# Four token-major projections in 512-column chunks, with their weights in a pool opened behind the ssd mixer

## The chip, the core and the metric

The kernel runs on one core of one Trainium2 chip. The metric is the device time of one launch in microseconds (us). The kernel before takes 2990.47 us, the median of three runs (2987.92 to 2991.99).

On a core, PE multiplies matrices, DVE does element-wise vector work, ACT does functions and copies, POOL does small odd jobs, and SP, ACT and POOL put DMAs into queues. Each engine works through its own list in order. A list may stop at a semaphore until another engine or a DMA has finished.

## The reference, cut to what matters

The reference is two transformer blocks in sequence over 1024 tokens of width 1024. The first has an RWKV-7 branch, a differential attention branch and a mixture of experts. The second, which the change touches, is this:

```python
h = rms_norm_2(x, pre_norm_w[l])
proj = h @ w_in[l]
z, xbc, dt_raw, q, f_raw, i_in, g, u, s5_gate = jnp.split(proj, splits, axis=-1)
y_ssd = ssd_mixer(z, xbc, dt_raw, ...)
y_hgrn = hgrn2_mixer(q, f_raw, i_in, g, ...)
y_s5 = s5_mixer(u, s5_gate, ...)
mix = jnp.concatenate([y_ssd, y_hgrn, y_s5], axis=-1)
x = x + rms_norm_2(mix @ w_out[l], post_norm_w[l])
```

The columns `i_in`, `g`, `u` and `s5_gate` are 512 wide each. Their products with `h` are the four products I0, G0, U0 and SG0 of the title; `g` and `s5_gate` pass through a SiLU.

## The kernel before, in words

All products keep float32 accuracy by splitting each operand into a high part (fp32r, made by a copy on ACT) and a low part (the difference, made on DVE). `mm3` then issues three matmuls for each block of 128 input rows: lines 262, 263 and 264. A product over 1024 input rows has 8 such blocks, so it takes 24 matmuls for each output tile.

`load_w` (line 208) brings weights in. For each part of `part` blocks it loads a raw tile by SP (`wr`, line 220, tag `wraw`), copies the high part on ACT (`wh`, line 181) and subtracts on DVE (`wl`, line 182). Each tag has a number of buffers; a new tile takes the buffer of an old one once all readers of that one are done.

The second block's input `h` lies transposed in SBUF as `hU` (high and low). There are two kinds of product with it:

- Feature-major (`proj_fm`, and the conv products of `ssd`): the output has features on partitions, and a matmul streams 512 tokens of `hU` past 128 columns of weights. The trace writes it `mm<-hU,wh`.
- Token-major (`proj_tm`, and the Z products of `ssd`): the output has 128 tokens on partitions, and a matmul streams CW columns of weights past 128 tokens of `hU`. The trace writes it `mm<-wh,hU`. With CW = 256, a product 512 wide is two chunks of 8 token tiles of 24 matmuls.

A chunk's weights are two parts of four blocks (128x1024 each), in a pool `wq` that all products of this stage share: two raw buffers and two each of `wl` and `wh`, which is one chunk.

`mixers` writes the second block in this order: `ssd` (conv products, Z products, and then a scan over eight chunks of 128 tokens, which is called chunk 0 to 7 below), then F0 and Q0 (feature-major), I0 and G0 (token-major), then the first three of four `hgrn` heads with U0 behind the first and SG0 behind the second, then the s5 mixer with the last head and the output projection.

That is the order of the program's text. The order on each engine is made when the program is built: a scheduler simulates the program and lets each engine take, of the instructions that are ready in its simulation, the one that the text has first. So instructions of the scan stand between those of F0, Q0, I0 and G0. Once built, the order on an engine is fixed, whatever the real times are.

One scan chunk is mostly DVE work. In turn: `y` from line 1408, then for each of two groups of eight heads the decay matrix `dec` (eight instructions of line 1418 on a loaded tile, exp on ACT at line 1419, a product with the scores from PE, line 1421, at line 1423), eight small matmuls with it (line 1426), a product with the state (line 1430), which DVE scales into `yo` (line 1432) and adds (lines 1433, 1434), an update of the state (matmul of line 1437, DVE lines 1439 and 1440), a gate (1443) with a sum of squares on ACT (1444). At the end of the chunk come a power on POOL (line 177), the scaling of `y` (line 1450), eight transposes on PE (line 1453), copies on ACT (line 1456) and a store. Lines 1406 and 1407 prepare the next chunk's `xdt` and `xw`.

Tiles live in pools that are opened and closed like a stack. The scan's pools (`sd_one` with its constants and the tokens `x_tm`, and `sd_wk`) are opened above `wq` and closed at the end of `ssd`.

Of the kernel before, what the change touches and what calls it, by code (L numbers as in the profile page):

```python
# [1458 lines left out]


LEVELS = (64, 32, 16, 8, 4, 2, 1)
CW = 256


def proj_tm(K, hT, wp, pool, c0, n, dst, silu=False):

    nc = K.nc
    for c in range(n // CW):
        w = K.load_w(wp, K.ap["w_in_2"][0], [(c0 + c * CW, CW)], raw_bufs=2)
        for j in range(8):  # L1470
            p = K.gemm_tm(w, hT, j, CW)
            z = pool.tile([128, CW], F32, name=K.name("pz"), tag="stage", bufs=3)
            evac(K, z, p[:, :CW], silu)
            nc.sync.dma_start(dst[j * 128:(j + 1) * 128, c * CW:(c + 1) * CW], z)


def proj_fm(K, hT, wp, pool, c0, n, dst, silu=False):

    nc = K.nc
    for f in range(n // 128):  # L1480
        w = K.load_w(wp, K.ap["w_in_2"][0], [(c0 + f * 128, 128)], part=KT, raw_bufs=2)
        for hf in range(2):
            p = K.gemm_fm(w, 0, 128, hT, hf * 512)
            z = pool.tile([128, 512], F32, name=K.name("pz"), tag="stage", bufs=3)
            evac(K, z, p, silu)
            nc.sync.dma_start(dst[f * 128:(f + 1) * 128, hf * 512:(hf + 1) * 512], z)


def evac(K, z, p, silu):
    if silu:  # L1490
        K.nc.scalar.activation(z, p, AF.Tanh, scale=0.5)
        K.nc.vector.scalar_tensor_tensor(z, z, 1.0, p, op0=OP.add, op1=OP.mult)
    else:
        K.nc.scalar.activation(z, p, AF.Copy)
# [540 lines left out]
def final_first(K, es, mixT_d, part_d):  # L2035


    nc = K.nc
    KF = 8
    fp = es.enter_context(K.pool(name="f1", bufs=1))  # L2040
    mv = mixT_d.rearrange("(k p) t -> p k t", p=128)
    for c in range(2):
        cs = slice(c * 512, (c + 1) * 512)
        w = K.resident(fp, K.ap["w_out_2"][0], 0, KF, cs, "f1w", raw_bufs=2)
        for j in range(8):
            rows = slice(j * 128, (j + 1) * 128)
            raw = fp.tile([128, KF, 128], F32, name=K.name("fr"), tag="fr", bufs=2)
            m = [fp.tile([128, KF, 128], F32R, name=K.name(f"fm{i}"), tag=f"fm{i}", bufs=2) for i in range(2)]
            nc.sync.dma_start(raw, mv[:, :, rows])
            K.split(m[0], m[1], raw)  # L2050
            p = K.gemm_tm(w, m, 0, 512, kt=KF)
            y = fp.tile([128, 512], F32, name=K.name("fy"), tag="fy", bufs=1)
            nc.scalar.activation(y, p, AF.Copy)
            nc.scalar.dma_start(part_d[rows, cs], y)
            yield
# [105 lines left out]
def mixers(K, es, hT, d5, mixT_d, part_d, x3_d, out):  # L2161

    tc = K.tc
    with K.pool(name="md", bufs=1, space=DRAM) as dd:
        wp, pool = [es.enter_context(K.pool(name=n, bufs=1)) for n in ("wq", "wqs")]
        dt = lambda n, *s: dd.tile(list(s), F32, name=f"d_{n}")
        zs_d, f_d, q_d, v_d = dt("zs", T, 1024), dt("f", 512, T), dt("q", 512, T), dt("v", T, 512)
        gh_d, u_d, g5_d = dt("gh", T, 512), dt("u", T, 512), dt("g5", T, 512)  # L2170
        ssd(K, hT, wp, pool, zs_d, mixT_d[0:1024, :], s5_tables(K, d5))
        a = (K, hT, wp, pool)
        proj_fm(*a, F0, 512, f_d)
        proj_fm(*a, Q0, 512, q_d, silu=True)
        proj_tm(*a, I0, 512, v_d)
        proj_tm(*a, G0, 512, gh_d, silu=True)
        heads = hgrn(K, f_d, q_d, v_d, gh_d, mixT_d[1024:1536, :])
        for h in range(3):
            next(heads)
            if h == 0:  # L2180
                proj_tm(*a, U0, 512, u_d)
            if h == 1:
                proj_tm(*a, SG0, 512, g5_d, silu=True)
        es.close()
        fs = ExitStack()
        last = Final(K, fs)
        first = final_first(K, fs, mixT_d[0:1024, :], part_d)

        def go(n, behind):
            with tc.issue_after(behind.ins):  # L2190
                for _ in range(n):
                    next(first)

        for _ in range(3):
            next(first)
        states = s5(K, d5, u_d, g5_d, last.open)
        next(states)
        next(heads)
        next(heads, None)
        for n in (2, 2, 2, 4):  # L2200
            next(states)
            go(n, K.last)
        for _ in states:
            mm = K.last
        end = last.run(mixT_d[1024:1536, :], part_d, x3_d, out)
        next(end)
        go(3, mm)
        next(end, None)
        fs.close()


def program(tc, nc, cst, out, **ap):
# [32 lines left out]
    pps.close()  # L2245
    rings.close()
    mixers(K, es, hT, d5, mixT_d, part_d, x3_d, out)
    K.close()

# [13 lines left out]
```

## Time and profile before

| | |
|---|---|
| time, median of three | 2990.47 us (2987.92 to 2991.99) |
| profiled execution | 2983.03 us |
| its span in the trace | 2981.3 us |
| PE busy | 2806.6 us, 94% |
| DVE busy | 1965.1 us, 66% |
| ACT busy | 1315.6 us, 44% |
| mean granted PE clock | 0.967 of full |

Matmuls are pipelined: each is longer than the distance to the next, so the busy time of PE is not its rate. The distance from start to start is. Times are read from the span's start. The second block begins near 2000 us, F0 runs from about 2265 us, Q0 ends at 2370.65 us, I0 and G0 follow until about 2497.5 us, U0 and SG0 until about 2641 us, and s5 and the output projection take the rest.

### The profile page before, as it was taken

What the parts mean: (1) busy time and instruction counts of PE and PEld (TensorE: products, weight loads), DVE (VectorE), ACT (ScalarE), POOL (GpSimd) and SP (SyncE); (2) the same over time, 40 slices, a digit from 0 to 9 for tenths busy, and PEclk for the clock granted to TensorE, in tenths of its full rate; (3) what the DMA queues carried; (4) which work ended last, traced back from release to release, by engine and by line L of the source; (5) the groups of instructions that cost most, each with busy time, mean ns of one, the idle gap of its engine ahead of it and who ended that gap; (6) DMA issues with size and microseconds to landing.
All of it is one profiled execution on the core that took longest, in us unless ns stands there. A gap on an engine that the chain in (4) does not pass through costs nothing. (4 is left out here: it accounts for less than half of the span.)

```text
span 2981.3 us, 47275 instructions
## 1 busy us (share of the span) xinstructions
PE 2806.6 (94%) x18410; PEld 2303.9 (77%) x18410; DVE 1965.1 (66%) x3826; ACT 1315.6 (44%) x2167; POOL 237.0 (8%) x193
## 2 busy tenths in 40 slices
PE   5999999998999989879999999899999999999998
PEld 4878888775777768668877777678888899987776
DVE  4436678744454655669989888469844676768653
ACT  3222223223454321568877878334432335543441
POOL 0000111100000000101222120000000000000000
PEclk9999999997899999889999999999999999999999
DMA  5333334323121655779999998442324444347333
GB/s 162 106 94 96 87 114 126 99 70 119 54 64 54 239 154 182 252 247 380 378 360 334 349 366 288 165 138 82 97 95 143 131 127 144 100 151 234 116 124 131
DMA packets 378146, 503.31 MB, mean 169 GB/s; under 512 B 86039, under 2 KB 234422, under 8 KB 377918
## 3 DMA queue, kind: packets, MB, share of 16 engines
q1 hardware_dynamic: 347742, 458.63, 46.7%
q0 software_dynamic: 11296, 24.57, 2.3%
q10 hardware_dynamic: 18880, 17.05, 1.7%
q8 instruction: 146, 2.39, 0.3%
q14 instruction: 82, 0.67, 0.1%
HBM read 410.26 MB, written 106.68 MB: 173 GB/s over the span
## 5 line engine op out<-in xcount | busy, mean ns | idle before, releaser
L182 DVE TENSOR_TENSOR wh<-we,wh 128x1024 fp32r<-128x1024 f32 x384 | 451.3, 1220 | 61.4 <-ACT wh L181 60.1
L181 ACT ACTIVATE wh<-we 128x1024 fp32r<-128x1024 f32 x384 | 386.1, 1057 | 50.0 <-PE b L264 29.7
L262 PE MATMUL mm<-wh,hU 128*128 128x256 f32 (+1 forms) x768 | 222.9, 292 | 6.8 <-DVE z L1363 4.1
L263 PE MATMUL mm<-wl,hU 128*128 128x256 f32 (+1 forms) x768 | 221.5, 289 | 2.5 <-DVE wl L182 2.5
L264 PE MATMUL mm<-wh,hU 128*128 128x256 f32 (+1 forms) x768 | 219.7, 287 | 0.0
L264 PE MATMUL mm<-wh,hT 128*128 128x256 f32 (+1 forms) x640 | 213.7, 335 | 0.0
L262 PE MATMUL mm<-wh,hT 128*128 128x256 f32 (+1 forms) x640 | 206.0, 338 | 2.7 <-ACT ye L1060 2.3
L262 PE MATMUL mm<-hT,wh 128*128 128x512 f32 x480 | 197.0, 410 | 4.4 <-DVE edge L309 4.2
L181 ACT ACTIVATE wh<-wr 128x1024 fp32r<-128x1024 f32 (+2 forms) x102 | 100.9, 992 | 208.4 <-PE mm L263 156.9
L264 PE MATMUL mm<-hT,wl 128*128 128x512 f32 x480 | 192.5, 401 | 0.0
L263 PE MATMUL mm<-hT,wh 128*128 128x512 f32 x480 | 192.1, 400 | 0.0
L182 DVE TENSOR_TENSOR wl<-wr,wh 128x1024 fp32r<-128x1024 f32 (+2 forms) x102 | 116.0, 1139 | 111.2 <-ACT wh L181 103.9
L262 PEld LDWEIGHTS mm<-wh,hU 128*128 128x128 f32 x768 | 147.2, 193 | 11.0 <-DVE z L1363 5.1
L263 PEld LDWEIGHTS mm<-wl,hU 128*128 128x128 f32 x768 | 148.0, 193 | 5.7 <-DVE wl L182 3.3
L264 PEld LDWEIGHTS mm<-wh,hU 128*128 128x128 f32 x768 | 148.0, 193 | 1.4 <-issue 1.4
L262 PEld LDWEIGHTS mm<-wh,hT 128*128 128x128 f32 x640 | 123.5, 194 | 21.5 <-issue 4.3
L264 PEld LDWEIGHTS mm<-wh,hT 128*128 128x128 f32 x640 | 124.0, 194 | 12.7 <-issue 1.5
L262 PE MATMUL mm<-hU,wh 128*128 128x512 f32 x320 | 128.5, 402 | 4.5 <-ACT wh L181 4.5
L263 PE MATMUL mm<-hU,wh 128*128 128x512 f32 x320 | 127.7, 399 | 0.0
L264 PE MATMUL mm<-hU,wl 128*128 128x512 f32 x320 | 126.9, 397 | 0.0
L262 PEld LDWEIGHTS mm<-hT,wh 128*128 128x128 f32 x480 | 92.5, 193 | 31.7 <-ACT xs L303 4.5
L263 PE MATMUL mm<-wl,hT 128*128 128x256 f32 x384 | 114.0, 297 | 1.3 <-DVE wl L182 1.3
(704 smaller groups left out, 7091.1 us busy)
## 6 DMA issues: line engine op xcount, KB each, us to landing
we<-w_gate SPq DMA_DIRECT2D x64, 1024.0 KB
we<-w_up SPq DMA_DIRECT2D x64, 1024.0 KB
we<-w_down SPq DMA_DIRECT2D x64, 1024.0 KB
wr<-w_in SPq DMA_DIRECT2D x86, 512.0 KB
d_gate<-gz SPq DMA_DIRECT2D x32, 256.0 KB
gt<-d_gate SPq DMA_DIRECT2D x16, 512.0 KB
x<-d_x SPq DMA_DIRECT2D x16, 512.0 KB
dec<-sd_cum SPq DMA_DIRECT2D x16, 512.0 KB
```

What stands on the lines that cost most here:

```text
L181: self.nc.scalar.activation(hi, src, AF.Copy)
L182: self.nc.vector.tensor_sub(lo, src, hi.bitcast(F32))
L262: nc.tensor.matmul(out, a[0], b[0], start=first, stop=False)
L263: nc.tensor.matmul(out, a[0], b[1], start=False, stop=False)
L264: self.last = nc.tensor.matmul(out, a[1], b[0], start=False, stop=last)
```

## The change

CW becomes 512, so that each of the four products is one chunk: 8 token tiles of 24 matmuls of 512 columns. A part is now two blocks of 512 columns (128x1024 again), a chunk has four parts, and `wl` and `wh` get four buffers each; the raw tiles keep two. The pool `wq` is closed behind Q0, and a new pool `wt` is opened for the four products. So that `wq` can be closed on its own, the pool of the output stage tiles (`wqs`) is opened ahead of it.

```diff
-CW = 256
+CW = 512
...
     for c in range(n // CW):
-        w = K.load_w(wp, K.ap["w_in_2"][0], [(c0 + c * CW, CW)], raw_bufs=2)
+        w = K.load_w(wp, K.ap["w_in_2"][0], [(c0 + c * CW, CW)], raw_bufs=2, bufs=4, part=2)
...
-        wp, pool = [es.enter_context(K.pool(name=n, bufs=1)) for n in ("wq", "wqs")]
+        pool = es.enter_context(K.pool(name="wqs", bufs=1))
+        ws = ExitStack()
+        wp = ws.enter_context(K.pool(name="wq", bufs=1))
...
         proj_fm(*a, F0, 512, f_d)
         proj_fm(*a, Q0, 512, q_d, silu=True)
+        ws.close()
+        a = (K, hT, es.enter_context(K.pool(name="wt", bufs=1)), pool)
         proj_tm(*a, I0, 512, v_d)
         proj_tm(*a, G0, 512, gh_d, silu=True)
```

The build of the program places the instructions anew. Four places show it. The number behind a name tells tiles apart; `mm_22470` is the last output tile of Q0, and the lines of the scan are those named above.

On PE before, from within the first tile of I0 (`mm_22511`), right behind Q0: the transposes of chunk 3 stand in the middle of the tile.

```order
L262 MATMUL mm_22511<-wh_22502,hU_17959 128x256
L263 MATMUL mm_22511<-wl_22500,hU_17959 128x256
L264 MATMUL mm_22511<-wh_22502,hU_17960 128x256
L1453 MATMUL t_21554<-c_ident,y_21473 128x128 [waits DVE_49,PE_49]
L1453 MATMUL t_21554<-c_ident,y_21473 128x128 x3
L1453 MATMUL t_21566<-c_ident,y_21473 128x128 [waits DVE_49]
L1453 MATMUL t_21566<-c_ident,y_21473 128x128 x3
L262 MATMUL mm_22511<-wh_22508,hU_17959 128x256 [waits Activation_49]
L263 MATMUL mm_22511<-wl_22506,hU_17959 128x256 [waits DVE_49]
```

On PE now, from the end of Q0 (`mm_22470`): the same transposes, and behind them chunk 4, of which the first ten rows are shown.

```order
L264 MATMUL mm_22470<-hU_17959,wl_22436 128x512
L1453 MATMUL t_21554<-c_ident,y_21473 128x128 [waits DVE_49,PE_49]
L1453 MATMUL t_21554<-c_ident,y_21473 128x128 x3
L1453 MATMUL t_21566<-c_ident,y_21473 128x128 [waits DVE_49]
L1453 MATMUL t_21566<-c_ident,y_21473 128x128 x3
L1421 MATMUL t_21598<-sd_c_fm,sd_b_fm 128x128 [waits Activation_49]
L1437 MATMUL t_21616<-xw_21578,sd_b_tm 128x512 [waits Activation_49]
L1426 MATMUL b_21601<-xdt_21577,dec_21587 128x64 [waits DVE_49]
L1426 MATMUL b_21601<-xdt_21577,dec_21587 128x64 x7
L1430 MATMUL b_21610<-prev_21479,sd_c_fm 128x512
L1421 MATMUL t_21633<-sd_c_fm,sd_b_fm 128x128 [waits PE_49]
L1437 MATMUL t_21651<-xw_21578,sd_b_tm 128x512 [waits DVE_49]
```

It goes on like this through chunks 4, 5, 6 and 7, with no product between. The next piece of PE now is the end of chunk 7 and the first two tiles of I0 (`mm_22527` and `mm_22555`).

```order
L1453 MATMUL t_21969<-c_ident,y_21897 128x128 [waits DVE_49]
L1453 MATMUL t_21969<-c_ident,y_21897 128x128 x3
L1453 MATMUL t_21981<-c_ident,y_21897 128x128 [waits DVE_49]
L1453 MATMUL t_21981<-c_ident,y_21897 128x128 x3
L262 MATMUL mm_22527<-wh_22506,hU_17959 128x512 [waits Activation_49]
L262 MATMUL mm_22555<-wh_22506,hU_17959 128x512
L263 MATMUL mm_22527<-wl_22504,hU_17959 128x512 [waits DVE_49]
L264 MATMUL mm_22527<-wh_22506,hU_17960 128x512
```

What moved: before, chunks 4 to 7 of the scan stand scattered among the matmuls of I0 and G0. Now all of them stand ahead of I0's first matmul.

On SP now, around the first weight loads of I0 (`wr_22503`, `wr_22509`), with the loads of the scan's last chunk ahead of them and those of the first hgrn head (`c_hglvl`, `fr`, `q`) behind.

```order
L1415 DMA dec_21904<-sd_cum 128x1024 [waits DVE_49,PE_49]
L1415 DMA dec_21935<-sd_cum 128x1024 [waits DMAHW6_49,DVE_49,PE_49]
L1405 DMA zs_21898<-d_zs 128x1024 [waits DMAHW7_49,DMAHW2_49,Activation_49]
L220 DMA wr_22503<-w_in 128x2x512 [waits DMAHW4_49]
L220 DMA wr_22509<-w_in 128x2x512 [waits DMAHW5_49]
L137 DMA c_hglvl<-consts 128x896 [waits DMAHW6_49,DVE_49]
L1525 DMA fr_23030<-d_f 128x1024 [waits DMAHW7_49]
L1526 DMA q_23031<-d_q 128x1024 [waits DMAHW0_49]
L1526 DMA q_23541<-d_q 128x1024 [waits DMAHW1_49]
L220 DMA wr_22515<-w_in 128x2x512 [waits DMAHW4_49,DMAHW2_49,DVE_49]
L220 DMA wr_22521<-w_in 128x2x512 [waits DMAHW5_49,DMAHW3_49,DVE_49]
```

What moved: before, the weight loads of I0 and G0 stand between the loads of chunks 4 to 7. Now they stand behind the last of them.

On DVE now, from the end of chunk 7 to the split of I0's third and fourth part.

```order
L1450 TENSOR_SCALAR y_21897<-y_21897,sst_21903 128x512 [waits DVE_49]
L182 TENSOR_TENSOR wl_22504<-wr_22503,wh_22506 128x1024 [waits DMAHW4_49,Activation_49]
L182 TENSOR_TENSOR wl_22510<-wr_22509,wh_22512 128x1024 [waits DMAHW5_49,Activation_49]
L1513 CAST hg_mask<-c_hglvl 128x512 [waits DMAHW6_49]
L1515 TENSOR_TENSOR hg_coarse<-c_ident,c_hglvl 128x128
L1515 TENSOR_TENSOR hg_coarse<-hg_coarse,c_hglvl 128x128 [waits DVE_49] x2
L1533 SCALAR_TENSOR_TENSOR lf_23032<-fr_23030,e_23033 128x1024 [waits DMAHW7_49,Activation_49]
L1534 TENSOR_TENSOR e_23033<-lf_23032,fr_23030 128x1024 [waits DVE_49]
L1537 SCALAR_TENSOR_TENSOR cum_23045<-hg_reset,lf_23032 128x1024
L182 TENSOR_TENSOR wl_22516<-wr_22515,wh_22518 128x1024 [waits DMAHW2_49,Activation_49]
L182 TENSOR_TENSOR wl_22522<-wr_22521,wh_22524 128x1024 [waits DMAHW3_49,Activation_49]
```

What moved: the splits of I0's weights stand behind the scan, and the first steps of hgrn head 0 stand between the second and the third.

## Rows read from the trace of the kernel before

**Rows 1.** The page's first line: span and instructions.

```profile
span 2981.3 us, 47275 instructions
```

**Rows 2.** Windows: us; busy of PE, PEld, DVE, ACT, POOL; PEclk, DMA, GB/s.

```profile
2371.00:2503.00 132.00, 127.08 (x992) 119.19 (x990) 82.17 (x150) 49.32 (x109) 2.78 (x4) 1.00 0.47 149
2503.00:2645.00 142.00, 140.33 (x1416) 137.10 (x1416) 104.74 (x159) 71.61 (x98) 4.92 (x4) 0.98 0.31 98
2645.00:2760.00 115.00, 107.14 (x804) 89.57 (x804) 94.81 (x167) 50.39 (x70) 4.76 (x4) 0.99 0.74 224
2373.51:2403.11 29.60, 29.60 (x232) 27.68 (x230) 20.05 (x38) 9.33 (x22) 0.69 (x1) 1.00 0.42 129
2434.46:2459.68 25.22, 23.59 (x176) 21.20 (x175) 19.73 (x41) 8.18 (x20) 0.69 (x1) 1.00 0.45 141
2459.68:2482.91 23.23, 23.23 (x189) 22.27 (x188) 13.28 (x22) 7.94 (x20) 0.70 (x1) 1.00 0.36 114
```

**Rows 3.** Timeline of PE, 512 columns to Q0's end, then 256: start, length.

```profile
2364.75 0.39 PE L263 MATMUL mm<-hU,wh 128*128 128x512 f32 x1
...
2370.43 0.39 PE L264 MATMUL mm<-hU,wl 128*128 128x512 f32 x1
...
2392.32 0.28 PE L262 MATMUL mm<-wh,hU 128*128 128x256 f32 x1
...
2398.31 0.28 PE L264 MATMUL mm<-wh,hU 128*128 128x256 f32 x1
```

**Rows 4.** Timeline of DVE, scan chunks 3 and 4, with idle before and releaser.

```profile
2369.16 0.88 DVE L1450 TENSOR_SCALAR y<-y,sst 128x512 f32<-128x512 f32 x2 [0.87 <-POOL sst L177]
...
2376.45 1.22 DVE L1423 TENSOR_TENSOR dec<-dec,t 128x1024 f32<-128x1024 f32 x1 [1.72 <-PE t L1421]
...
2382.93 0.69 DVE L1432 TENSOR_TENSOR yo<-b,sd_ecum 128x512 f32<-128x512 f32 x1 [4.11 <-PE b L1430]
...
2393.09 2.19 DVE L1418 SCALAR_TENSOR_TENSOR dec<-dec,sd_cum,sd_cap 128x128 f32<-128x128 f32 x8 [1.15 <-DMA dec<-sd_cum]
```

**Rows 5.** Groups by line, 2376 to 2503: count, busy, mean ns, idle before.

```profile
L1426 PE MATMUL b<-xdt,dec 128*128 128x64 f32 x128 | 15.2, 272 | 0.0
...
L182 DVE TENSOR_TENSOR wl<-wr,wh 128x1024 fp32r<-128x1024 f32 x8 | 9.8, 1224 | 4.3 <-ACT wh L181 4.1
...
L1430 PE MATMUL b<-prev,sd_c_fm 128*128 128x512 f32 x16 | 8.6, 616 | 1.3 <-DVE y L1434 1.3
L181 ACT ACTIVATE wh<-wr 128x1024 fp32r<-128x1024 f32 x8 | 8.5, 1061 | 3.1 <-PE mm L264 3.1
L1492 DVE SCALAR_TENSOR_TENSOR pz<-pz,mm 128x256 f32<-128x256 f32 x16 | 6.6, 418 | 15.5 <-ACT pz L1491 15.0 <-DMA d_gh<-pz 0.5
...
L1437 PE MATMUL t<-xw,sd_b_tm 128*128 128x512 f32 x12 | 6.1, 593 | 0.0
...
L1453 PE MATMUL t<-c_ident,y 128*128 128x128 f32 x32 | 4.1, 273 | 0.0
...
L1421 PE MATMUL t<-sd_c_fm,sd_b_fm 128*128 128x128 f32 x16 | 3.1, 272 | 0.0
```

**Rows 6.** Timeline of PE at the start of U0, behind a wait for weights.

```profile
2502.98 0.79 PE L262 MATMUL mm<-wh,hU 128*128 128x256 f32 x2 [2.19 <-ACT wh L181]
2503.57 0.41 PE L263 MATMUL mm<-wl,hU 128*128 128x256 f32 x1
...
2508.26 0.41 PE L264 MATMUL mm<-wh,hU 128*128 128x256 f32 x1
```

**Rows 7.** Timeline of SP and ACT: the start of hgrn head 0.

```profile
2490.38 0.42 SPq L1525 DMA_DIRECT2D fr<-d_f  x1
...
2494.69 1.06 ACT L1530 ACTIVATE e<-fr 128x1024 f32<-128x1024 f32 x1 [2.28 <-DMA fr<-d_f]
...
2497.93 1.28 ACT L1532 ACT_TABLE_LOAD   x1
```

**Rows 8.** Timeline of PE where the second block's products begin.

```profile
2004.10 0.79 PE L262 MATMUL mm<-hU,wh 128*128 128x512 f32 x1 [4.51 <-ACT wh L181]
```

## The prediction

> **What bounds the kernel now.** I read the page's first line for the span [rows 1], then windows over the stages that the change touches. There the reader is to see PE busy for 127.08 of 132 us in I0 and G0 and for 140.33 of 142 us in U0 and SG0, while DVE is busy for 82 and 105 us [rows 2]. PE is never long without work in these stages. What keeps it so is the mixture: the ssd scan's chunks are chains in which DVE waits for PE and PE for DVE, and the products fill PE in between. A shorter product therefore shortens the program only if the scan still has something to hide behind. The timelines of PE and DVE then give the pace of the matmuls and of a chunk.
>
> **The change part by part.** Six terms, each against the profiled execution of 2983.03 us (span 2981.3 [rows 1], 1.7 us around it).
>
> *a) The scan loses its cover.* On PE all of chunks 4 to 7 now stand ahead of I0's first matmul, with no product between. So the time from Q0's end to I0's start is the time of these four chunks alone. Q0's last matmul starts at 2370.43, the next would at 2370.65 [rows 3]. Chunk 3's last scaling ends at 2369.16 + 0.88 = 2370.04 [rows 4]. Chunk 4's first DVE instruction came at 2373.51 behind a weight split of 1.22 us [rows 2, 5]; that split is gone, so it starts near 2372.4.
>
> How long is a chunk without products beside it? Before, it took 29.60 us for chunk 4 and 25.22 for chunk 6 [rows 2]. From below: DVE was busy for 20.05 us in chunk 4, of which 1.22 is a weight split, so 18.8 us is what DVE needs if it never waits. From above: 29.6, as before. Chunk 6 had a weight split and four evacuations (about 1.6 us together, 0.42 each, overlapping [rows 5]) that now are gone: 25.2 - 2.8 = 22.4. Against that, PE will be idle for several us at a time, and this trace shows what follows: behind a wait of 2.19 us the matmuls of U0 come every (2508.26 - 2503.57) / 22 = 0.213 us instead of 0.120, the lower of the clock's two levels, 1.2 GHz [rows 6, 3]. Part of the chunk's PE work stands on its chain (DVE waits 1.72 us for the scores and 4.11 us for the state product in chunk 4 [rows 4]); I add 3 us for it at the lower level part of the time, and take 25.5, nearest to chunk 6's row. Chunk 7 has no next chunk to prepare: its 23.23 us held 13.28 of DVE work, of which two splits and six evacuations are 4.9 [rows 2, 5]. I take 16.5, between 13 and 23.2.
>
> The end is 2372.4 + 3 x 25.5 + 16.5 = 2465.4, and 1.1 us later the transposes are done. I0's first split on ACT stands behind the copies of these transposes (1.6 us still to run) and takes 1.06 [rows 5], so I0 starts near 2469.2. From 2370.65 that is 98.5 us. In it PE does the scan's own work, which before stood inside the window of I0 and G0: 15.2 + 8.6 + 6.1 + 4.1 + 3.1 [rows 5], and 1.0 for chunk 3's transposes, 38.1 us. Lost: 60.4 us. With 18.8 and 13 it is 36.8, with 29.6 and 23.2 it is 79.4.
>
> *b) I0's second half.* Parts one and two feed 24 matmuls, 5.4 us. There are two raw buffers, so part three's load waits for the first split on DVE, ends some 4.3 us later (as `fr` did, 2490.38 to 2494.69 [rows 7]), and its split on DVE is queued behind the first steps of hgrn head 0, which need `fr` and three ACT steps with a table load of 1.28 us first. By these, `fr` lands near 2470.3, ACT's steps end at 2474.6, three DVE steps (1.2, 1.2, 2.3) and the split (1.2) at 2480.4, while PE is through at 2474.7. Cost 5.7 us; from 2 to 10.
>
> *c) Wider matmuls.* 256 columns start every (2398.31 - 2392.32) / 50 = 0.1198 us, 512 every (2370.43 - 2364.75) / 25 = 0.2272 [rows 3]. Two for one saves 0.0124 us; 4 products x 8 tiles x 24 = 768 pairs, 9.5 us. PE sets the end in these stages, so all of it counts. No row shows 512 columns at the lower level here; if the gain vanishes there it is 8, so from 8 to 10. The Trainium skill, "TensorE: Matmul & The Clock Gate", section "Wait — 56ns, not 53.3ns?", says that matmuls in a row start N / 2.4 GHz plus about 2.5 ns apart when warm, so two for one would save 2.5 ns and the four products 1.9 us (an estimate): the sum would be 7.6 us more. The trace has 12.4 ns, and is used.
>
> *d) Chunk boundaries.* Before, PE waits 132 - 127.08 and 142 - 140.33 us, 6.6 us, mostly for weight splits where a chunk ends, and 23 matmuls after one such wait cost 23 x 0.093 = 2.1 us more at the lower clock [rows 2, 6]. I let all 8.7 us go and put 1 us back at each of the starts of G0, U0 and SG0: there the first two parts of the next product are split while the last tile still runs, and two tiles share these parts until the others come. -5.7; from -8.7 to +8 (each start as dear as I0's).
>
> *e) The seam in front.* With `wqs` first, `wq` lies elsewhere, and the first conv weights stand behind the last norm's transposes on PE, ACT and DVE. PE already waits 4.51 us there [rows 8]. +2; from 0 to +5, the wait once more.
>
> *f) The hgrn heads.* Head 0 starts beside I0 now, but head 2, of which a part ran beside SG0, now falls behind it, into a stretch where DVE is busy for 94.81 of 115 us [rows 2]. +5; from 0 to +12. More splits or evacuations there are none: as many elements are split and evacuated, in instructions of the same size or twice it, and POOL has nothing new.
>
> Sum: 60.4 + 5.7 - 9.5 - 5.7 + 2 + 5 = 57.9. On the profiled 2983.03 that is 3040.9. That execution lies 7.4 below the median of the runs, 2990.47, so I forecast 2990.5 + 57.9 = 3048.4.
>
> **The rivals.**
>
> *The clock stays up.* The scan alone keeps PE at 2.4 GHz: the windows of these stages show a granted clock of 1.00 and 0.98 [rows 2]. Against it, their PE was full, and 2.19 us of idling was enough once. Then a chunk is 22.4 and the last 14.5, I0 starts at 2457.9, a is 49.1 and the time 3037.
>
> *The clock stays down through the scan.* All of PE's 38.1 us run at half rate; 7 us of each chunk fall on its chain, so a chunk is 29.4, the last 20, I0 starts at 2484.4, a is 75.6 and the time 3064. For it: rows 6. Against it: there the clock was back after some 5 us of matmuls. The Trainium skill says the same of idle gaps in "TensorE: Matmul & The Clock Gate", section "HAM oscillation — how this bites in real kernels": each gap puts the array back to half rate for the start of the next burst. Rows 6 agree for one such gap.
>
> *The boundaries are dear.* Two raw buffers for four parts let every product start like I0, three more stalls of 5.7 in place of 1: 3062. For it: a chunk had all its raw tiles ahead before, and has half now. Against it: the shared first parts give 5.4 us.
>
> *Not slower: the heads run ahead.* hgrn head 0 starts beside I0. If by SG0's end the heads are one head further than before, 25 to 35 us of DVE work (104.74 us in a stage that holds some two and a half heads [rows 2]) leave the stretch behind it, where PE idles too: the sum loses f's 5 and up to 35, 3008. It ends below the time before only if the scan also runs at DVE's floor, a = 36.8: then 57.9 - 40 - 23.6 = -5.7, 2985. It decides from a below 43. Against it: PE takes products before heads, as the text has them first, so a head beside G0 gets little of PE.
>
> That the four products stay in chunks of 256, or the scan between them, the order excludes.
>
> **How the numbers follow.** Forecast 0.40, clock up 0.25, clock down 0.18, boundaries 0.12, heads ahead 0.05. The forecast's own terms reach from 3035 to 3062. With the rivals on both sides and a at its ends, the range is 3026 to 3070. A measurement of this kernel tells 0.2%, 6 us, from no change. All cases but the last lie over 40 us above; of the last I give 0.02 to faster and 0.01 to no change.
>
> **What would show it.** In the profile after: PE with idle stretches and a lower granted clock for about 100 us behind Q0, and DVE the busier engine there; a chunk, from one instruction of line 1408 to the next, of 24 to 27 us (a: 22 or 29 tell the rivals); one PE wait of 4 to 8 us in I0 for `wl` (b); 512-column matmuls 0.227 us apart in the four products (c); no PE wait over 2 us at the starts of G0, U0 and SG0 (d); the first conv matmul 0 to 5 us later (e); PE idle behind SG0 up by some us (f). I am wrong if products stand between the chunks on PE, if a chunk takes under 20 us, or if the stretch behind SG0 shrinks by more than 10.

## The result and the profile after

The changed kernel is slower: 3068.46 us against 2991.23 us, medians of four runs each, a ratio of 1.0262 (95% interval 1.0245 to 1.0278), which is 77.2 us. The forecast was 57.9 us. Its profiled execution took 3069.81 us.

Three lines of its page, to be laid beside the table of before and [rows 1]: the span, the busy time of each engine with its share and instructions, and the granted clock in forty equal slices.

```profile
span 3068.0 us, 45569 instructions
PE 2832.4 (92%) x17642; PEld 2280.0 (74%) x17642; DVE 1965.1 (64%) x3810; ACT 1313.0 (43%) x2135; POOL 236.3 (8%) x193
...
PEclk9999989996999998989999999999999679999999
```

DVE does the same work to a tenth of a microsecond. PE has fewer instructions and a longer busy time, and two neighbouring slices (2378 to 2531 us) have a clock of 6 and 7 tenths: the place of the change.

The windows below are the stretches that answer to [rows 2]: four chunks of the scan, each from one line 1408 to the next (the last to the end of line 1450), then from I0's first matmul to SG0's last, then to the first load of the s5 mixer. Columns as in [rows 2].

```profile
2388.70:2413.20 24.50, 11.41 (x52) 7.21 (x52) 18.68 (x37) 5.85 (x16) 0.69 (x1) 0.72 0.29 97
2413.20:2441.00 27.80, 15.91 (x52) 10.07 (x52) 18.69 (x36) 5.74 (x16) 0.69 (x1) 0.56 0.24 76
2441.00:2466.00 25.00, 13.17 (x46) 8.66 (x47) 17.57 (x34) 4.91 (x12) 0.69 (x1) 0.64 0.22 74
2466.00:2487.50 21.50, 14.54 (x50) 10.41 (x49) 8.92 (x13) 3.62 (x12) 0.69 (x1) 0.50 0.55 180
...
2492.00:2715.60 223.60, 220.43 (x1276) 182.80 (x1276) 113.84 (x157) 88.20 (x103) 4.93 (x4) 0.98 0.31 103
2715.60:2777.40 61.80, 53.50 (x514) 46.42 (x512) 52.00 (x84) 38.37 (x53) 2.39 (x2) 0.89 0.54 171
```

Before, PE was busy all through chunk 4 (29.60 of 29.60 us [rows 2]). Now it is busy for 11 to 16 us of a chunk, at a clock of 0.50 to 0.72. Chunks 4 to 7 took 29.60, 31.35, 25.22 and 23.23 us before and take 24.50, 27.80, 25.00 and 21.50 now: 10.6 us less in all, with no product beside them. The window of chunk 5 before is this:

```profile
2403.11:2434.46 31.35, 31.35 (x245) 29.33 (x243) 21.13 (x39) 10.36 (x26) 0.69 (x1) 1.00 0.43 136
```

The timeline of PE over chunk 5 shows what is left on PE:

```profile
2413.57 0.79 PE L1421 MATMUL t<-sd_c_fm,sd_b_fm 128*128 128x128 f32 x2 [0.38 <-ACT syT L1456]
2414.60 2.07 PE L1437 MATMUL t<-xw,sd_b_tm 128*128 128x512 f32 x2 [0.24 <-ACT syT L1456]
2416.47 3.51 PE L1426 MATMUL b<-xdt,dec 128*128 128x64 f32 x16
2419.77 2.02 PE L1430 MATMUL b<-prev,sd_c_fm 128*128 128x512 f32 x2
...
2423.70 2.00 PE L1426 MATMUL b<-xdt,dec 128*128 128x64 f32 x16
2427.60 2.08 PE L1430 MATMUL b<-prev,sd_c_fm 128*128 128x512 f32 x2 [1.89 <-DVE y L1434]
2439.04 1.94 PE L1453 MATMUL t<-c_ident,y 128*128 128x128 f32 x8 [9.37 <-DVE y L1450]
```

Where products stood there is a wait of 9.37 us. The eight matmuls of line 1426 that a group has (sixteen rows of the trace, which shows an fp32 matmul as two) take 3.51 us a few us behind such a wait and 2.00 us a little later. The Trainium skill tells in "TensorE: Matmul & The Clock Gate", section "HAM oscillation — how this bites in real kernels", of a kernel in which the wait for a DMA in every tile puts the array back to half rate, so that each next tile starts slow; the trace agrees, with 3.51 and 2.00 us.

To see where time went, I add up PE's timeline from Q0's last matmul to the first load of s5, from each start to the next, less the idle time that stands before it. All are us of one execution each; the parts can miss the sum by 0.7 (1.5 where the same is done for a run below).

| | before | changed | changed again | cover lost, 256 wide | the same again |
|---|---|---|---|---|---|
| products | 197.7 | 184.7 | 184.2 | 192.5 | 192.2 |
| hgrn heads | 61.0 | 64.7 | 64.6 | 67.6 | 67.5 |
| scan | 27.2 | 57.7 | 56.2 | 57.6 | 56.0 |
| first s5 and output matmuls | 22.5 | 25.1 | 25.3 | 24.0 | 22.6 |
| idle while the scan is alone | 0 | 47.0 | 48.8 | 47.5 | 48.8 |
| idle otherwise | 11.7 | 11.2 | 14.2 | 5.5 | 6.9 |
| Q0's end to I0's start | 0.2 | 104.9 | 105.2 | 105.4 | 105.0 |
| I0's start to s5's first load | 319.7 | 285.4 | 288.2 | 288.8 | 288.3 |

The row "Q0's end to I0's start" rests on Q0's last matmul, which before started at 2370.43 [rows 3], and on I0's first:

```profile
2387.07 0.39 PE L264 MATMUL mm<-hU,wl 128*128 128x512 f32 x1
...
2492.00 1.22 PE L262 MATMUL mm<-wh,hU 128*128 128x512 f32 x2 [2.91 <-ACT wh L181]
```

From Q0's end to s5's first load it is 390.3 us now and 320.0 before: 70.3 us. Another 5.0 us come earlier, at the seam in front of `ssd`. And at the load of `sd_rows`, near 2009 us, the two profiles are already 11.7 us apart; the twelve profiles of the experiments stand between -0.4 and 13.0 us there, so nearly all of that is the execution's, not the change's (at the last matmul `mm<-we,hj`, ahead of the seam, it is 11.0, so up to 0.7 more may be the seam's). The change's are 70.3 + 5.0 = 75.3 us, and what lies behind adds nothing (87.1 us apart at s5's first load, 86.8 at the last store).

### The profile page after: what moved, and what is told of

Read it like the earlier page. It is cut to its first block, busy times and chain, and to the rows that moved or that the text cites. A ratio compares the mean times of both kernels' runs of the same rounds, so it can differ in the third digit from the quotient of the medians.

```text
span 3068.0 us, 45569 instructions
## 1 busy us (share of the span) xinstructions
PE 2832.4 (92%) x17642; PEld 2280.0 (74%) x17642; DVE 1965.1 (64%) x3810; ACT 1313.0 (43%) x2135; POOL 236.3 (8%) x193
## 5 line engine op out<-in xcount | busy, mean ns | idle before, releaser
L181 ACT ACTIVATE wh<-we 128x1024 fp32r<-128x1024 f32 x384 | 386.1, 1057 | 48.3 <-PE b L264 27.8
L263 PE MATMUL mm<-hT,wh 128*128 128x512 f32 x480 | 192.5, 401 | 0.2 <-DVE hT L206 0.2
L262 PE MATMUL mm<-wh,hU 128*128 128x512 f32 (+2 forms) x512 | 176.4, 347 | 8.7 <-DVE z L1363 3.7
L263 PE MATMUL mm<-wl,hU 128*128 128x512 f32 (+2 forms) x512 | 175.4, 343 | 1.7 <-DVE wl L182 1.7
L264 PE MATMUL mm<-wh,hU 128*128 128x512 f32 (+2 forms) x512 | 174.4, 341 | 0.0
L262 PEld LDWEIGHTS mm<-wh,hU 128*128 128x128 f32 x512 | 97.7, 192 | 20.6 <-DVE z L1363 4.7
L264 PEld LDWEIGHTS mm<-hT,wl 128*128 128x128 f32 x480 | 92.6, 193 | 20.4 <-issue 0.4
L263 PEld LDWEIGHTS mm<-wl,hU 128*128 128x128 f32 x512 | 98.1, 192 | 12.9 <-DVE wl L182 2.8
```

Source lines behind the costliest of these rows:

```text
L181: self.nc.scalar.activation(hi, src, AF.Copy)
L262: nc.tensor.matmul(out, a[0], b[0], start=first, stop=False)
L263: nc.tensor.matmul(out, a[0], b[1], start=False, stop=False)
L264: self.last = nc.tensor.matmul(out, a[1], b[0], start=False, stop=last)
```

## The experiments

Ratios are to the kernel before on the same chip, with 95% intervals.

| run | ratio | interval |
|---|---|---|
| stage pool first, nothing else | 1.0007 | 0.9996 to 1.0019 |
| pools moved, 256 wide, small pool | 1.0056 | 1.0034 to 1.0078 |
| pools moved, 256 wide, 40 KB pool | 1.0271, again 1.0248 | 1.0249 to 1.0294, 1.0222 to 1.0274 |
| changed kernel again | 1.0245 | 1.0219 to 1.0271 |
| only U0 and SG0 wide | 1.0029 | 1.0016 to 1.0042 |
| the same, heads first | 1.0007 | 0.9992 to 1.0022 |
| kernel before, heads first | 1.0006 | 0.9993 to 1.0019 |
| changed kernel, heads first | 1.0236 | 1.0221 to 1.0252 |
| changed kernel, scan filled | 1.0320 | 1.0302 to 1.0337 |
| gap filled late | 1.0267 | 1.0249 to 1.0286 |
| gap filled early | 1.0226 | 1.0204 to 1.0248 |

**The seam.** The order of the two pools alone:

```diff
-        wp, pool = [es.enter_context(K.pool(name=n, bufs=1)) for n in ("wq", "wqs")]
+        pool, wp = [es.enter_context(K.pool(name=n, bufs=1)) for n in ("wqs", "wq")]
```

> The kernel before with one edit: the stage pool wqs is opened ahead of wq; products stay 256 wide and stay among the scan's chunks. Theory (the seam is dearer than forecast: in the profile after PE waits 8.9 us for the last norm and 1.6 for the conv weights, before 4.5): 4 to 7 us over the kernel before, 2995 to 2998, and at the first conv matmul PE waits 8 to 10 us for the last norm instead of 4.5 for a weight. Rival (the later times ahead of Q0 in the profile after are only one execution's clock): within 2 us of the kernel before, and the PE wait at the seam near 4.5.

The waits of PE at the seam (engine, line, who is waited for: us, times, longest) in this run:

```profile
PE t L202 <- DVE h L192: 8.9, 1, 8.9
PE mm L262 <- ACT wh L181: 1.6, 1, 1.6
```

and in the run with only U0 and SG0 wide, which keeps the old order of the pools:

```profile
PE mm L263 <- ACT wh L181: 4.5, 1, 4.5
```

Before, the first conv matmul was ready behind a wait of 4.51 us [rows 8], ahead of the last norm's transposes; now PE waits 8.9 us for these first. Every profile with the new order loses 5.2 to 5.8 us between the load of `sd_rows` and the first store of Z against the kernel before (5.0 are left at Q0's end in the changed kernel); the three with the old order lose nothing (-0.5 to 0). The whole time of this run does not show it apart from noise: its interval reaches from -1.2 to 5.7 us. So the loss at the seam is shown; that all of it arrives at the end is not.

**What takes the cover away.** The pools as in the changed kernel, but 256 columns and two buffers as before, so that `wt` is no larger than `wq` was:

```diff
-CW = 512
+CW = 256
...
-raw_bufs=2, bufs=4, part=2)
+raw_bufs=2)
```

> The pools are opened and closed as in the changed kernel, but the products stay 256 wide with two raw and two split buffers, so that the new pool is no larger than the old one. The scan's chunks 4 to 7 then have 142, 190, 138 and 154 products' matmuls between them on PE. Theory (what loses the cover is that 40 KB per partition reach over the scan's own tiles): 5 to 12 us over the kernel before, 2996 to 3003, of which 4 to 7 are the seam. Rival (any pool that opens behind the scan waits for it): 3065 or more.

It was 16.8 us (10 to 23) over the kernel before: far from 3065, but more than I expected. I0's first matmul comes 7 us behind Q0's last, where before it was the next: the first weight load is issued 2.9 us ahead of Q0's last matmul, before it was 6.0 us. In its trace the seam costs 5.6 us and the way from Q0's end to s5's first load 7.8 more than before. Then the same with 16 KB more in the pool:

```diff
+        wt = es.enter_context(K.pool(name="wt", bufs=1))
+        gap = wt.tile([128, 4096], F32, name="gap")
+        K.nc.vector.memset(gap[:, 0:1], 0.0)
+        a = (K, hT, wt, pool)
```

> As the run with moved pools and 256-wide products, but the new pool is made 40 KB large by an unused 16 KB tile at its bottom. Chunks 4 to 7 have no product between them again. Theory (cover is the whole loss, the width is a gain of 9.5 us, and the two more boundaries of 256-wide chunks cost 0 to 8): 3075 to 3086, so slower than the changed kernel. Rival (the wide chunks, their four parts and two raw buffers are a good part of the loss): under 3060.

1.0271, in us 81 (75 to 88): the whole loss of the changed kernel (77.2) within the noise, with matmuls as narrow as before. The last two columns of the table above are this kernel; up to I0's start it agrees with the changed one to 0.5 us. So the loss belongs to the size of the pool, not to the width. In the program's memory map `wq`'s room ends at byte 115,456 of a partition, where the scan's constants begin, and `x_tm` follows at 116,768. The four `wh` buffers of `wt` lie from 113,920 to 130,304, on top of both, and the scan reads these until its last chunk. Why the loads are late as well, whose raw buffers end at 97,536, no run settles.

**The price of the width.** The changed kernel and the narrow one with the cover lost, on one chip:

> The changed kernel itself, for a comparison on the same chip with the runs beside it: 1.0245 to 1.0278 of the kernel before. Each theory expects the same of it.

> The run with the cover lost and 256-wide products, beside the changed kernel on the same chip, to price the width alone. Theory (in the traces the products take 192.5 us at 256 columns and 181.8 at 512, and the wide kernel gives 7.7 us of it back as PE waits): 2 to 6 us over the changed kernel. Rival (all of the 10.7 us arrive): 9 to 13 us over. Other rival (all is given back): within 2 us.

1.0245 and 1.0248: no difference, but the intervals are 8 us to either side, so by the times alone none of the three expectations falls. In both pairs of traces the products are 7.8 and 8.0 us shorter at 512 columns, the heads' matmuls 2.9. But 5.7 and 7.3 us come back as idle time of PE and 1.1 and 2.7 us as longer matmuls of s5 and the output product, and 3.4 and 0.1 us are left: between theory's lower end and the rival that all is given back, and far from the rival that all arrives.

**Width where the cover is kept.** U0 and SG0 alone are wide. Their first two parts lie in `wq`, the last two in a pool `wx` that opens behind the first head:

```diff
-    def load_w(self, pool, w, segs, kt=KT, raw_bufs=1, bufs=2, part=4):
+    def load_w(self, pool, w, segs, kt=KT, raw_bufs=1, bufs=2, part=4, more=None):
...
+            wp = more if more is not None and k0 >= kt // 2 else pool
...
             if h == 0:
-                proj_tm(*a, U0, 512, u_d)
+                more = es.enter_context(K.pool(name="wx", bufs=1))
+                proj_tm(*a, U0, 512, u_d, more=more)
```

> The kernel before, with U0 and SG0 alone 512 wide. Their first two weight parts lie in the old pool, the other two in a 16 KB pool that is opened behind the first hgrn head, so I0 and G0 cover the scan as before and nothing at the seam changes. Theory (wide is a gain where the cover is kept): 2 products x 8 tiles x 24 pairs x 0.0124 = 4.8 us, and 0 to 3 us of the waits at chunk boundaries: 2983 to 2987. Rival 1 (the gain of width is not on the path, or the hgrn heads give it back): within 2 us of 2991. Rival 2 (each wide product starts with a stall of some 5 us for its second half): 2994 to 2998.

8.7 us slower than before (4.8 to 12.6): theory fell. Its products are 6.5 us shorter (191.2 against 197.7; but in the other traces with 256 columns and the cover kept they take 195.3 to 196.5, so 4 to 6.5 us is nearer the mark), and idle time rises from 11.7 to 22.4 us. The waits of PE from 2500 to 2640 us in this run:

```profile
PE mm L264 <- DVE wl L182: 5.2, 2, 4.4
PE mm L263 <- ACT wh L181: 3.2, 3, 2.3
PE mm L263 <- ACT pz L1496: 1.1, 1, 1.1
```

Half of it, 4.9 us, is U0's second half, as the second rival said: two raw buffers for four parts, and the splits queued behind the first head. Another 3.4 us are waits for the splits of its first half. The other loss stands behind SG0: 63.9 us to s5's first load instead of 50.1. There 198 head matmuls are left by the built order, where before had 105 and the changed kernel has 196.

**Heads first.** So I wrote U0 behind the second head and SG0 behind the third, in three kernels:

```diff
-            if h == 0:
+            if h == 1:
                 proj_tm(*a, U0, 512, u_d)
-            if h == 1:
+            if h == 2:
                 proj_tm(*a, SG0, 512, g5_d, silu=True)
```

> The changed kernel with U0 written behind the second hgrn head and SG0 behind the third, instead of behind the first and second. Behind the last product PE then has 83 head matmuls left instead of 196 (kernel before: 105). Theory (with 512-wide products the third head is pushed behind SG0, and that stretch is 13 us longer for it): from SG0's last store to s5's first loads 45 to 50 us instead of 60, and the time 8 to 15 us under the changed kernel, 1.022 or less of the kernel before. Rival (the stretch is long for another reason, or products slowed by the heads give it back): within 4 us of the changed kernel.

> The kernel with U0 and SG0 alone 512 wide, and with U0 written behind the second head and SG0 behind the third: 96 head matmuls are left behind the last product instead of 198. Theory (width itself gains 5 us, and the run before lost 13 in the stretch behind SG0): 10 to 14 us under that run, 0 to 6 us under the kernel before. Rival (the loss of that run is U0's later start): no change against it, 1.003 of the kernel before.

> The kernel before, 256 wide, with U0 written behind the second head and SG0 behind the third; 75 head matmuls are left behind the last product instead of 105. Theory (what is left behind the last product sets that stretch, and PE is full ahead of it): 0 to 5 us under the kernel before. Rival (heads in front hold PE up for DVE among the products): 2 to 10 us over.

The stretch behind SG0 did shrink in the changed kernel, from 61.8 to 43.3 us. But SG0's end came later, and from I0's start to s5's first load it is 285.9 us, as without the edit (285.4 and 288.2). The time is 1.0236, under the 1.0262 of the changed kernel, within the interval of its rerun, and over the 1.022 of theory. The wide U0 and SG0 gained 6.6 us by it, half of what I expected (the two intervals just overlap), and end level with the kernel before; in its trace the same way fell from 329.2 to 326.7 us, and the products took 195.4 us, no less than the 195.6 of the narrow ones in the same order. The kernel before gained nothing, and its way grew from 319.7 to 324.9. So a shorter stretch behind SG0 is not a gain as it stands: it is largely paid for ahead of SG0's end.

**The clock in the scan.** Throwaway matmuls in chunks 4 to 7, first in seven places of a chunk:

```diff
+        def fill(src):
+            if j >= 4:
+                pf = K.ps(tag="a")
+                for _ in range(2):
+                    nc.tensor.matmul(pf, K.ident, src, start=True, stop=True)
+
+        fill(xw[:, 0:512])
...
+            if j >= 4:
+                fill(prev[:, gs])
...
+                fill(dec[:, 0:512])
...
+                fill(yo)
```

> The changed kernel with throwaway matmuls in chunks 4 to 7 of the scan: seven places a chunk, two fp32 matmuls of 512 columns each, into a free PSUM tag that nobody reads, some 1.9 us a place at full clock. They keep PE's clock up where the profile after has 0.50 to 0.72. Theory (about a tenth of the scan's length is the low clock on its chain): granted clock over 0.9 in the chunks, chunks of 21 to 23 us instead of 24.5 to 27.8, and 8 to 16 us under the changed kernel. Rival (the chain is DVE's, the clock costs nothing): chunk lengths as in the changed kernel or longer, time within 4 us or above.

The clock rose (1.00, 0.83, 0.80 and 0.80), but the chunks took 26.6, 29.9, 29.5 and 22.0 us, for the fillers stood in the way: line 1426 of the second group came behind two of them. The time, 1.0320, is as the rival said; since the fillers lengthen the chain themselves, this says nothing on the price of the clock. Next only the gap ahead of the transposes:

```diff
+                if j >= 4 and g == 1:
+                    fill(dec[:, 0:512])
...
+                if j >= 4 and g == 1:
+                    fill(yo)
...
+            if j >= 4 and g == 1:
+                fill(zs[:, gs], 3)
```

with two on the next `xw` as before.

> As the filled run, but throwaway matmuls only in the gap of some 9 us that PE has in the changed kernel between a chunk's second state product and its transposes: nine fp32 matmuls of 512 columns a chunk, 0.94 us each at full clock, behind nothing that the chain needs (they read dec, yo, the squares and the next xw). Theory (the low clock lengthens the chain: DVE waits 4.4 us for the state product where 2.9 would do at full clock, and the scores and transposes likewise): granted clock over 0.85 in the chunks, chunks of 21.5 to 24 us instead of 24.5 to 27.8, 6 to 14 us under the changed kernel run beside it. Rival (only the order of the chain counts): chunks as long as before, within 3 us of it.

DVE in chunk 5 of this run; line 1408 begins a chunk, 1442 and 1464 are 1432 and 1450 of the changed kernel:

```profile
2404.49 1.23 DVE L1408 TENSOR_TENSOR y<-sd_x_tm,sd_rows 128x1024 f32<-128x1024 f32 x1 [5.17 <-PE t L1467]
2410.09 0.69 DVE L1442 TENSOR_TENSOR yo<-b,sd_ecum 128x512 f32<-128x512 f32 x1 [1.96 <-PE b L1438]
...
2426.34 0.88 DVE L1464 TENSOR_SCALAR y<-y,sst 128x512 f32<-128x512 f32 x2 [0.87 <-POOL sst L177]
2433.79 1.23 DVE L1408 TENSOR_TENSOR y<-sd_x_tm,sd_rows 128x1024 f32<-128x1024 f32 x1 [6.57 <-PE t L1467]
```

and in the changed kernel:

```profile
2413.22 1.23 DVE L1408 TENSOR_TENSOR y<-sd_x_tm,sd_rows 128x1024 f32<-128x1024 f32 x1 [1.73 <-PE t L1453]
2421.83 0.69 DVE L1432 TENSOR_TENSOR yo<-b,sd_ecum 128x512 f32<-128x512 f32 x1 [4.43 <-PE b L1430]
...
2438.41 0.88 DVE L1450 TENSOR_SCALAR y<-y,sst 128x512 f32<-128x512 f32 x2 [0.87 <-POOL sst L177]
2441.02 1.23 DVE L1408 TENSOR_TENSOR y<-sd_x_tm,sd_rows 128x1024 f32<-128x1024 f32 x1 [1.73 <-PE t L1453]
```

The way from 1408 to the scaling fell from 25.2 to 21.9 us, and the wait for the state product from 4.43 to 1.96; then the transposes were 5 us late behind fillers that had waited for the squares. So chunks 4 and 5 took 27.7 and 29.3 us at a clock of 0.94 and 0.88, and the time was 1.0267: theory fell for both, and only the way inside the chunk shows what the clock is worth. So, last, fillers that read what is early:

```diff
+        if j >= 5:
+            fill(xw[:, 0:512], 3)
...
+                if j >= 4 and g == 1:
+                    fill(yo, 2)
...
+            if j >= 4 and g == 0:
+                fill(y[:, gs], 3)
```

> As the run with the filled gap, but the throwaway matmuls read what is ready early (half of y, yo, the next xw: 3, 2 and 3 of them), so that they end before the transposes are due; there the ones on the squares waited for ACT and held the transposes up by 5 to 6.6 us, while the way from line 1408 to line 1450 had already come down from 25.2 to 21.9 us in chunk 5. Theory (the low clock costs some 3 us a chunk on the chain): DVE waits about 2 us instead of 4.4 for the state product, chunks of 22 to 24 us, 6 to 12 us under the changed kernel, 1.021 to 1.024 of the kernel before. Rival (the gain is given back elsewhere): 1.0245 or more.

Windows over chunks 4, 5 and 6 of this run:

```profile
2389.64:2413.33 23.69, 17.91 (x68) 9.72 (x68) 18.65 (x37) 5.41 (x14) 0.69 (x1) 0.93 0.31 100
2413.33:2440.53 27.20, 24.07 (x68) 13.14 (x68) 18.76 (x36) 5.73 (x15) 0.69 (x1) 0.69 0.24 77
2440.53:2463.20 22.67, 17.87 (x68) 9.82 (x68) 17.55 (x34) 5.78 (x15) 0.69 (x1) 0.92 0.30 95
```

With a clock of 0.92 and 0.93 a chunk takes 22.7 and 23.7 us, with 0.69 it takes 27.2. That is not the clock alone: chunk 5 is the longest of the four in the kernel before too, and chunk 6 has 1.2 us less DVE work. DVE's wait for the state product, chunk 5 and then chunk 6 (line 1440 here), is the clock's part:

```profile
2422.35 0.69 DVE L1440 TENSOR_TENSOR yo<-b,sd_ecum 128x512 f32<-128x512 f32 x1 [4.43 <-PE b L1438]
...
2446.14 0.69 DVE L1440 TENSOR_TENSOR yo<-b,sd_ecum 128x512 f32<-128x512 f32 x1 [1.96 <-PE b L1438]
```

With the wait for line 1437's product (1.08 and 0.45 us) that is 3.1 us, close to the 3.3 us by which the way inside chunk 5 got shorter in the run before. Against the same chunks of the changed kernel chunks 4 to 7 are 0.8, 0.6, 2.3 and 1.6 us shorter, and Q0's end to I0's start is 99.2 us instead of 104.9 to 105.4, 5.7 us less, though chunks 5 and 7 kept a low clock (0.69 and 0.66). The time, 1.0226, lies where theory put it, but its interval overlaps that of the changed kernel's rerun, 1.0245, and the spans of the two traces are level (3067.8 and 3068.0 us): behind s5's first load this one is 3.5 us longer, in the same code (the other traces scatter by 10 us there). So the gain is shown in the scan, not at the end.

## Why the prediction came out as it did

The mechanism was forecast and found: the scan runs alone for some 100 us behind Q0. The size was some 18 us short, and 3068.46 lies 1.5 us inside the upper end of the range, 3070. By steps:

*a) The scan loses its cover: 60.4 forecast, 77.7 measured (104.9 less 27.2), near the end of its bounds, 79.4.* Two sizes were wrong. Three chunks took 24.5, 27.8 and 25.0 us (forecast 25.5 each, 0.8 us too little in sum, and the 3 us that I had added in each for the lower clock are what the filled runs show); the last took 21.5, not 16.5, since DVE waits in it 2.90 us for the scores, 4.45 and 3.41 us for the two state products, at a clock of 0.50. Having no next chunk to prepare saves DVE work, but that was not what bounded it. I0 starts 104.9 us behind Q0's last matmul, 6.4 more than forecast. The other 10.9 us are an error of reckoning: I credited PE with 38.1 us of scan work that before stood among the products. That is the sum of busy times [rows 5], and matmuls overlap; from start to start it was 27.2 us. The same text warns of this for products and counts those by their distance. With that alone put right the forecast is 3059.

*b) I0's second half: 5.7 forecast, 3.1 measured, by another wait.* The waits of PE inside I0:

```profile
2502.53 2.05 PE L1545 MATMUL a<-q,k 128*128 128x128 f32 x16 [1.05 <-ACT k L1535]
...
2511.69 0.50 PE L262 MATMUL mm<-wh,hU 128*128 128x512 f32 x1 [2.08 <-ACT pz L1494]
```

The third part's split ended 11.2 us behind I0's start, as reckoned, and was there in time all the same: the matmuls of the first parts took until 2501.5, which is 9.5 us and not 5.4, half of them at the lower clock (0.43 us apart), and head 0's first matmuls stood behind them. PE waited for these head matmuls' `k` on ACT and for an evacuation on ACT instead. The wait that I had described came where the weights are loaded late without the scan to hide it, in U0 of the run with only U0 and SG0 wide.

*c) Wider matmuls: -9.5 forecast.* The cadence was right:

```profile
2520.24 0.39 PE L262 MATMUL mm<-wh,hU 128*128 128x512 f32 x1
...
2529.76 0.39 PE L262 MATMUL mm<-wh,hU 128*128 128x512 f32 x1
```

42 matmuls in 9.52 us are 0.2267 each, and the products are 7.8 to 8.0 us shorter than the narrow ones with the cover lost, 1.5 us less than forecast. What failed is the sentence that PE sets the end there, so that all of it counts: from I0's start to s5's first load the width is worth 3.4 us in one pair of traces and 0.1 in the other, and nothing that the times show. The 1.9 us worked out (an estimate) from the Trainium skill, "TensorE: Matmul & The Clock Gate", section "Wait — 56ns, not 53.3ns?", are off as a price of the matmuls: these traces have 12.4 ns for each pair.

*d) Boundaries: -5.7.* Behind the wait at 2511.69 and up to 2720 us, where G0, U0 and SG0 start, the trace lists no wait of PE, as forecast. What that is worth by itself no run shows, for the way from I0's start to s5's first load holds it together with c.

*e) The seam: 2 forecast, 5.0 measured.* I had the bound of 5 from a second wait of the size of [rows 8]. What grew was the first wait, 8.9 us for the norm.

*f) The hgrn heads: 5 forecast.* The waits behind SG0 after, from 2715.6 to 2777.4 us, are these:

```profile
PE a L1559 <- DVE lv L1554: 3.9, 1, 3.9
PE mm L262 <- ACT fm L181: 2.2, 2, 1.7
PE b L1590 <- ACT kt L1586: 1.0, 1, 1.0
PE mm L262 <- ACT f1w L181: 0.9, 1, 0.9
```

and before (2640.3 to 2690.4 us) the three longest of five are these:

```profile
PE mm L262 <- ACT fm L181: 2.7, 2, 1.6
PE b L1590 <- DVE hst L1592: 1.4, 1, 1.4
PE mm L262 <- ACT f1w L181: 1.2, 1, 1.2
```

The stretch is 11.7 us longer (61.8 against 50.1), twice the forecast, with 196 head matmuls instead of 105 left behind the last product. But b, c, d and f can't be told apart by these runs: the way from I0's start to s5's first load holds them all, and with the heads written first it stayed as long. Together they were forecast at -4.5 us. From I0's start to s5's first load it is 285.4 us now and was 319.7 - 27.2 = 292.5 before: -7.1. The rerun has 288.2, -4.3. In sum that part was near, by terms that were not: that is luck.

In all: a 17.3 us more than forecast, e 3.0 more, the rest 2.6 less: 17.7, which with 57.9 is 75.6; measured were 75.3 in the traces and 77.2 in the medians.

*The rivals.* "The clock stays down through the scan" came nearest, with a chunk of 29.4, a last one of 20 and 3064: chunks were 24.5 to 27.8, so only the last was near what it said, and its time came near by luck too, since it credits the same 38.1 us. "The clock stays up" fell: 0.50 to 0.72 was granted. "The boundaries are dear" fell for the changed kernel. "The heads run ahead" fell; they fall behind. Of what I had named as signs, the idle PE, the chunk of 24 to 27 us in two of three (24.5 and 25.0, not 27.8), the cadence, the starts without waits and the longer stretch behind SG0 were there; the wait for `wl` in I0 was not, and the first conv matmul came 7.3 us later (2023.08 against 2004.10, less the 11.7 us that the executions were apart).

The low clock's share is shown in size: some 3 us in a chunk whose first state product runs at the lower clock. What stays open is why from I0's start to s5's first load about 286 to 289 us are needed at either width and in either order of the heads, with PE idle for 5.5 to 14.2 us of them; and how much of the seam's 5 us, and of what the fillers gain, arrives at the end.

## What to carry to other kernels

A larger buffer that is opened behind a stage can reach over that stage's own memory, and then what was its cover stands behind it: look at where a pool lies before reckoning what its tiles are worth. Count work that leaves a full engine by the distance from start to start, for the sum of busy times credits overlapped work twice (38.1 for 27.2 us here). A gain on the busiest engine need not arrive: of 8 us of shorter products 0.1 to 3.4 us were left in the traces here, and nothing that the times show. The rest came back as idle time of PE and as longer matmuls elsewhere; why, no run here settles.

## What the runs showed of the hardware

PE's clock fell where its work thinned, with no wait longer than 9.4 us: the granted clock was 0.50 to 0.72 over 99 us in which PE was busy for 47 to 68% of a chunk. Behind such waits eight fp32 matmuls of 64 columns (sixteen rows of the trace) took 3.51 us, at full clock 1.89 (in the filled runs). Throwaway matmuls raised it: eight in a window of a chunk, of 512 columns in fp32, brought 0.93 and 0.92 in two chunks of the three, and 0.69 in the third. The scan got shorter (by 5.7 us) only in the run in which they ended before the chain needed PE; in the two runs in which they did not, the time was 1.0267 and 1.0320 of the kernel before, no better than without them.
